# Splitting the q and k weight columns by the halves of the heads' dims, and storing the gate sums from ScalarE's queue, in a hybrid attention block

## The chip, the cores and the metric

The kernel runs on one core of a Trainium2 chip. The metric is the device time of one launch in microseconds; lower is better. Five engines work side by side, each with its own queue of instructions in order: TensorE (PE, matrix products; its weight loads are listed as PEld), VectorE (DVE), ScalarE (ACT), GpSimd (POOL) and SyncE (SP, which here only issues transfers). A transfer is issued by an instruction in an engine's queue (SPq, ACTq) and carried out by 16 DMA engines.

## The reference, cut to what matters

One encoder layer on x of 1024 rows by 1024 columns, all in 32-bit floats. What the change touches is the first product and the rope:

```python
h_in = rms_norm(x, norm_mix_g[l], NORM_EPS)
proj = h_in @ w_in[l]
qa, ka, va, qb, kb, vb, ga, gb = jnp.split(proj, split_idx, axis=-1)
qa = apply_rope(qa.reshape(b, s, A_HEADS, HEAD_DIM), cos, sin)   # the same for ka, qb, kb
...
def apply_rope(t, cos, sin):                                     # heads of 64 dims
    rot = jnp.concatenate([-t4[..., HALF_DIM:], t4[..., :HALF_DIM]], axis=-1)
    out = t4 * cos[None, :, None, :] + rot * sin[None, :, None, :]
```

qa, ka, qb and kb are 512 columns each, the gates ga and gb 1024 each. After that come dilated and differential attention, the gates, an output product, an MLP of 4096 and a last norm; the change leaves these alone but for the addresses from which attention reads q and k.

## The kernel before

Every large product is a Strassen product: a 256-column block of weights is cut into a11, a12, a21, a22 (upper or lower 512 rows of either 128-column half), and seven smaller products of 512 rows replace eight. Each product is twelve matmuls on TensorE (`product`, L245), since every operand is split into a high part (`_h`, made by ScalarE in `halves`, L253) and a low remainder (`_l`, L254, made by GpSimd, or by VectorE for `wd_`), and three of the four cross products are taken. The result is transposed: 128 output columns on the partitions, 1024 rows along the free side.

The change is in stage 1, which makes q, k, v and the gates, and above all in its loop over sixteen items: eight pairs of q or k tiles (`qk_pair`; pairs 8, 12, 10, 14, 0, 4, 2, 6) and eight gates (`gate_rest`; 4, 5, 6, 7, 0, 1, 2, 3), by turns, except that the last four are q2, q6, g2, g3. An item takes five products in `rest_products`. Two go into a double PSUM bank `y` (operands s2 and s4, names `yq` or `yg`), two into a double bank `z` (s1 and s3; `zq`, `zg`), one into a bank of its own (a4; `4q`, `4g`). The pairs 0, 4, 2 and 6 take their two first products (`f0q`, `f1q`) there too, from an operand `wa_q`; those of 8, 12, 10 and 14 (`qk_early`) and of the gates are made elsewhere. The y and the z bank are each there twice, so a bank is taken again two items later, once VectorE has evicted it (L297 for y, L303 for z, L306 for the last).

The operands of one item stand in three buffers per part that go round: `ws_` (s2, s4), `wd_` (s1) and `wt_` (s3, a4). The sums behind them (L273 to L276) are VectorE's, and read the raw columns that SP has loaded two items ahead (L259).

A finished pair goes through `rope` behind the item that follows it in the program. For each of its two tiles, four transfers between blocks of 32 partitions (L501) make the copy `rot` with the halves of every head changed over; then VectorE multiplies rot by the signed sine (L502), GpSimd the tile by the cosine (L503), VectorE adds (L504), ScalarE takes the high part (L512) and VectorE the low (L513), and ScalarE's queue stores both (L514, L515). A finished gate leaves three tiles of sums, `gc`, which SP's queue stores to `gp` (L547), each behind the eviction that completes it. Differential attention begins behind the loop, with SP's loads `kb` and `qb` (L670, L676) and the scores `sb` (L697).

The program order on each engine is not that of the text: a planner of the tile framework puts the instructions of each engine in a row.

Of the kernel before, what the change touches and what calls it, by code (L numbers as in the profile page):

```python
# [37 lines left out]
def shape_tables():  # L38
# [8 lines left out]
    sin_t = np.concatenate([-sin, sin, -sin, sin], 0)  # L47
# [36 lines left out]
def tile_hybrid_block(ctx: ExitStack, tc: tile.TileContext, t: dict, out: bass.AP):  # L84
# [100 lines left out]
    qk_d = [dram(f"qk{j}", [2, P, S]) for j in range(16)]  # L185
# [84 lines left out]
    def rest_operands(name, ra, rb, s1):  # L270

        a11, a12, a21, a22 = ra[:, :DK, :], ra[:, DK:, :], rb[:, :DK, :], rb[:, DK:, :]
# [3 lines left out]
        nc.vector.tensor_tensor(a12, a12, a11, op=ALU.subtract)  # L276
        s2, s4 = halves(ra, f"ws_{name}")
# [218 lines left out]
    def rope(j, raw):  # L496
        scale = -0.125 if j % 8 < 4 else 1.0
        rot = big("xn", f"rot{j}", 2)
        for b in range(4):
            o = b ^ 1  # L500
            nc.sync.dma_start(rot[32 * b:32 * b + 32, :], raw[32 * o:32 * o + 32, :])  # L501
        nc.vector.scalar_tensor_tensor(rot, rot, scale, sin_t, op0=ALU.mult, op1=ALU.mult)  # L502
        nc.gpsimd.tensor_tensor(raw, raw, cos_t, op=ALU.mult)  # L503
        nc.vector.scalar_tensor_tensor(raw, raw, scale, rot, op0=ALU.mult, op1=ALU.add)  # L504
        hi, lo = [big("rh", f"r{z}_{j}", 2, F32R) for z in range(2)]
        if j < 4:

# [18 lines left out]
    def qk_pair(j, raws):  # L526
        xa, xb = [big("x", f"raw{j + a}", 4) for a in range(2)]
        p, u = [p1.tile([P, 512], F32, tag="p1", name=f"{nm}{j}", bufs=4) for nm in ("qp", "qu")]
        if j in EARLY:
            for z, x in enumerate((p, xa[:, 0:512])):  # L530
                nc.sync.dma_start(x, early_d[EARLY.index(j)][z])
        else:
            a11, a12 = halves(raws[0], f"wa_q{j}")
            first_products(f"q{j}", a11, a12, p, xa[:, 0:512])
        operands = rest_operands(f"q{j}", *raws, s1_tile(f"q{j}"))
        rest_products(f"q{j}", operands, p, u, (xa[:, 512:], xb[:, :512], xb[:, 512:]), lambda *_: None)
        return lambda: (rope(j, xa), rope(j + 1, xb))
# [4 lines left out]
    def gate_rest(n, raws):  # L542
        u = p1.tile([P, 512], F32, tag="p1", name=f"gu{n}", bufs=4)
        dst = [p1.tile([P, 512], F32, tag="x", name=f"gc{n}{k}", bufs=4) for k in range(3)]

        def done(a, b, c):
            nc.sync.dma_start(part_d[n][2 * a + b - 1], c)  # L547

        rest_products(f"g{n}", rest_operands(f"g{n}", *raws, s1_tile(f"g{n}")), None, u, dst, done)

    GATES = (4, 5, 6, 7, 0, 1, 2, 3)
    todo = []
    for j, n in zip(EARLY + (0, 4, 2, 6), GATES):
# [46 lines left out]
    def load_qk(jq, jk, half, name):  # L600

        r = slice(64 * half, 64 * half + 64)
        q_src = qk_d[jq][:, r, :].rearrange("z d s -> d z s")
        k_src = [bass.AP(tensor=a.tensor, offset=a.offset, ap=[[S, 64], [0, 2], [1, S]])
                 for a in (qk_d[jk][0, r, :], qk_d[jk][1, r, :])]
# [57 lines left out]
    def b_open(h):  # L663
# [4 lines left out]
        for m in range(2):  # L668
            k = p2q.tile([P, S], F32R, tag="qk", name=f"kb{h}_{m}", bufs=NQK)
            nc.sync.dma_start(f(k), qk_d[12 + h][:, 64 * m:64 * m + 64, :].rearrange("z d s -> d z s"))  # L670
            o.k.append(k)
        for half in range(2):
            for m in range(2):
                q = p2q.tile([P, 2, 512], F32R, tag="qk", name=f"qb{h}_{m}_{half}", bufs=NQK)
                for z in range(2):
                    nc.sync.dma_start(  # L676
                        f(q)[:, z, :], dup(qk_d[8 + h][z, 64 * m:64 * m + 64, 512 * half:512 * half + 512]))
# [789 lines left out]
```

## Time and profile before

| | |
|---|---|
| three runs | 1678.48, 1679.65, 1672.11 us; median 1678.48 |
| the profiled execution, its own time | 1671.93 us, with a span of 1670.1 us |
| granted TensorE clock, mean | 0.974 of full speed |
| TensorE busy in the span | 1560.1 us, 93% |
| VectorE, ScalarE, GpSimd busy | 71%, 42%, 35% |
| stage 1 before the loop; the loop; up to the scores at work | 0 to 139.2; 139.2 to 422.7; 422.7 to 440 us |

How to read it: the table of the loop is the place to look, since nothing else is rewritten. Inside it, the end of each pair's fifth product (the last `4q` matmul) is a mark: the distance from one mark to the next is the time of one pair and one gate. A timeline row gives the start, the duration, the engine, the line, and in brackets the idle time ahead of it and what ended that.

### The profile page before, as it was taken

How to read it: one execution, taken by the hardware profiler on the slowest of the kernel's cores; microseconds unless marked ns; L12 is line 12 of the kernel's file. 1: busy time of each engine (PE TensorE's matmuls, PEld its weight loads, DVE VectorE, ACT ScalarE, POOL GpSimd, SP SyncE). 2: the span in 40 equal slices, each digit the busy share in tenths (PEclk: the TensorE clock that was granted, in tenths of full speed). 3: DMA queues.
4: the chain of work that ended last, by engine and by line, in shares of the span. 5: the costliest groups of instructions: out<-in, count | busy, mean ns of one | idle time of the engine just before them, and what ended most of it. 6: DMA issues, size and time to landing. Idle time of an engine off the chain costs nothing. (4 is left out here: it accounts for less than half of the span.)

```text
span 1670.1 us, 21713 instructions
## 1 busy us (share of the span) xinstructions
PE 1560.1 (93%) x8216; PEld 1319.2 (79%) x8216; DVE 1187.1 (71%) x1383; ACT 698.7 (42%) x1064; POOL 577.1 (35%) x289
## 2 busy tenths in 40 slices
PE   8899889998789997989999999899999998999998
PEld 7798767766677886988878998688888777888876
DVE  5977888699688996655537447644444599899984
ACT  4432222222566873544432326444444552333332
POOL 2644444555232331021220004433333234354551
PEclk9999999999999998999999999999999999999999
DMA  6366576555866657656557332444333561413112
GB/s 230 113 222 199 175 231 201 171 187 158 276 195 212 224 195 269 198 169 216 166 164 277 117 112 88 127 129 130 101 101 114 191 243 46 167 68 124 51 38 101
DMA packets 218488, 271.28 MB, mean 162 GB/s; under 512 B 12784, under 2 KB 145040, under 8 KB 218384
## 3 DMA queue, kind: packets, MB, share of 16 engines
q1 hardware_dynamic: 204560, 236.33, 44.1%
q10 hardware_dynamic: 13824, 33.56, 5.3%
q8 instruction: 65, 1.06, 0.3%
q14 instruction: 39, 0.32, 0.1%
HBM read 183.81 MB, written 80.27 MB: 158 GB/s over the span
## 5 line engine op out<-in xcount | busy, mean ns | idle before, releaser
L1356 PE MATMUL p<-b,a 128*128 128x512 f32 x392 | 155.8, 398 | 5.3 <-DVE b L1272 5.3
L1355 PE MATMUL p<-b,a 128*128 128x512 f32 x392 | 155.3, 396 | 4.4 <-ACT a L1271 4.4
L1357 PE MATMUL p<-b,a 128*128 128x512 f32 x392 | 155.3, 397 | 0.9 <-DVE a L1272 0.9
L1272 POOL TENSOR_TENSOR b<-ws,b 128x1024 fp32r<-128x1024 f32 x27 | 79.1, 2943 | 128.3 <-ACT b L1271 118.3
L1356 PEld LDWEIGHTS p<-b,a 128*128 128x128 f32 x392 | 74.7, 191 | 23.1 <-DVE b L1272 5.7
L1355 PEld LDWEIGHTS p<-b,a 128*128 128x128 f32 x392 | 74.6, 190 | 21.5 <-ACT a L1271 4.9
L1357 PEld LDWEIGHTS p<-b,a 128*128 128x128 f32 x392 | 74.7, 191 | 18.1 <-DVE a L1272 1.5
L697 PE MATMUL sb<-kb,qb 128*128 128x512 f32 x256 | 75.0, 417 | 13.7 <-ACT p L702 8.1
L702 ACT ACTIVATE p<-sb,mn 128x1024 f32<-128x1024 f32 x64 | 71.2, 1115 | 37.4 <-DVE mn L700 23.5
L700 DVE TENSOR_REDUCE mn<-sb 128x1 f32<-128x1024 f32 x64 | 76.8, 1218 | 9.0 <-PE sb L697 8.7
L273 DVE TENSOR_TENSOR s<-w 128x512 f32<-128x512 f32 x15 | 16.9, 1125 | 85.6 <-DMA w<-in_w_ff 85.6
L164 POOL TENSOR_SCALAR n_y<-n_ss 128x1 f32<-128x1 f32 x23 | 6.3, 274 | 188.6 <-ACT n_xn L171 187.1
L811 PE MATMUL sa<-kh_a,zq 128*128 128x256 f32 x256 | 69.1, 301 | 0.9 <-DVE mna L820 0.8
L836 DVE TENSOR_TENSOR pta<-ta,pta 128x512 fp32r<-128x512 f32 x64 | 43.8, 688 | 33.9 <-ACT pta L835 33.8
L1271 ACT ACTIVATE a<-fs 128x1024 fp32r<-128x1024 f32 x28 | 29.4, 1054 | 91.0 <-PE p L1356 64.8
L697 PEld LDWEIGHTS sb<-kb,qb 128*128 128x128 f32 x256 | 46.2, 194 | 26.4 <-ACT p L702 12.4
L811 PE MATMUL sa<-kl_a,zq 128*128 128x256 f32 x256 | 65.9, 288 | 0.0
L254 POOL TENSOR_TENSOR wt_f_l<-w,wt_f_h 128x1024 fp32r<-128x1024 f32 x15 | 36.1, 2405 | 83.7 <-ACT wt_f_h L253 83.7
L1143 ACT ACTIVATE c<-c 128x512 f32<-128x512 f32 x64 | 40.0, 624 | 47.7 <-DVE c L300 35.6
L824 ACT ACTIVATE sm<-sm,mna 128x512 f32<-128x512 f32 x64 | 46.1, 720 | 32.5 <-DVE mna L820 32.0
L835 ACT ACTIVATE pta<-ta 128x512 fp32r<-128x512 f32 x64 | 37.6, 591 | 52.1 <-PE ta L831 44.4
L641 POOL TENSOR_TENSOR gq<-gq,gp 128x512 f32<-128x512 f32 x24 | 36.1, 1533 | 59.4 <-ACT gp L636 59.4
(497 smaller groups left out, 5117.2 us busy)
## 6 DMA issues: line engine op xcount, KB each, us to landing
w<-in_w_in SPq DMA_DIRECT2D x32, 512.0 KB, 4.3
qk<-r ACTq DMA_DIRECT2D x32, 512.0 KB, 5.3
f<-c ACTq DMA_DIRECT2D x64, 256.0 KB, 2.0
rb<-in_w_ff SPq DMA_DIRECT2D x32, 512.0 KB, 5.5
ra<-f SPq DMA_DIRECT2D x64, 256.0 KB, 4.9
w<-in_w_ff SPq DMA_DIRECT2D x30, 512.0 KB, 4.4
vb<-vb SPq DMA_DIRECT2D x16, 512.0 KB, 6.6
rot<-raw SPq DMA_DIRECT2D x64, 128.0 KB, 4.4
```

What stands on the lines that cost most here:

```text
L697: nc.tensor.matmul(sps[:, 512 * n:512 * n + 512], q[:, z, (qb % 4) * P:(qb % 4 + 1) * P], o.k[m][:, 512 * n:512 * n + 512], start=z == 0, ...
L700: nc.vector.tensor_reduce(mn, sps, axis=AX.X, op=ALU.min)
L702: nc.scalar.activation(p, sps, AF.Exp, scale=-1.0, bias=mn, accum_out=o.zz[qb][:, m:m + 1])
L811: nc.tensor.matmul(ps[:, 0:CM], zq[:, n % 4, c, :], kk[:, c * CM:(c + 1) * CM], start=c == 0 and kk is o.kh, stop=c == NCLS - 1 and kk is ...
L824: nc.scalar.activation(sm, sm, AF.Exp, scale=-1.0, bias=mn, accum_out=stat[h % 2][:, n:n + 1])
L835: nc.scalar.activation(view[0], tv, AF.Copy)
L836: nc.vector.tensor_tensor(view[1], tv, f(view[0]), op=ALU.subtract)
L1143: nc.scalar.activation(c, c, AF.Relu)
L1272: eng.tensor_tensor(lo, x, f(hi), op=ALU.subtract)
L1355: nc.tensor.matmul(acc, ah[:, i % 2, c], bh[:, i % 2, :], start=i == 0 and not more, stop=False, skip_group_check=bool(more))
L1356: nc.tensor.matmul(acc, ah[:, i % 2, c], bl[:, i % 2, :], start=False, stop=False, skip_group_check=bool(more))
L1357: nc.tensor.matmul(acc, al[:, i % 2, c], bh[:, i % 2, :], start=False, stop=last, skip_group_check=bool(more))
```

## The change

The raw columns of a pair of q or k tiles were loaded as two blocks of 1024 rows and 128 columns, one for each tile (two heads). They are now loaded as two blocks of 512 rows and 256 columns (four heads), and a tile's operand is picked from them as every other group of 32 columns: `xa` gets the first halves of four heads, `xb` the second halves. The rope then needs no copy between partitions: both tiles are multiplied by sine and cosine, GpSimd making the two products of `xb`, and combined crosswise. The 64 `rot` transfers of 128 KB are gone; the number of arithmetic instructions of a pair's rope stays (VectorE six, GpSimd two, ScalarE two), as does the number of stores. The `rot` tiles are used again for the low parts. In DRAM, q and k rows keep their order head by head, which the stores see to.

With the cut by rows, ws_ now holds s2 and s3, and wt_ holds s4 and a4. The early pairs load 2 blocks of 512 KB instead of one each, 2 MB more in all.

The 24 gate stores are issued by `nc.scalar` instead of `nc.sync`.

```diff
-    sin_t = np.concatenate([-sin, sin, -sin, sin], 0)
+    sin_t = np.concatenate([sin] * 4, 0)
...
-    qk_d = [dram(f"qk{j}", [2, P, S]) for j in range(16)]
+    qk_d = [dram(f"qk{j}", [2, 2 * P, S]) for j in range(8)]
...
+    def qk_raw(j, name, slot):
+        return [v_raw_at(512 * k, qk_col(j), f"{name}{k}", *slot) for k in range(2)]
...
+    def qk_blocks(r):
+        x = r.rearrange("p k (h s i) -> p (k h) s i", s=2, i=32)
+        return [x[:, :, z, :] for z in range(2)]
+    def qk_first(raws, name, eng):
+        hi = wp.tile([P, DC, P], F32R, tag="wh", name=name + "_h", bufs=3)
+        lo = wp.tile([P, DC, P], F32R, tag="wl", name=name + "_l", bufs=3)
+        for k, r in enumerate(raws):
+            x = qk_blocks(r)[0]
+            to_hi, to_lo = [z[:, DK * k:DK * k + DK, :].rearrange("p k (h i) -> p (k h) i", i=32) for z in (hi, lo)]
+            nc.scalar.activation(to_hi, x, AF.Copy)
+            eng.tensor_tensor(to_lo, x, f(to_hi), op=ALU.subtract)
...
+    def qk_halves(r, name):
...
+        x = r.rearrange("p k (h s i) -> p (k h) s i", s=2, i=32)
+        to_hi, to_lo = [z.rearrange("p (s k) (h i) -> p (k h) s i", s=2, i=32) for z in (hi, lo)]
+        nc.scalar.activation(to_hi, x, AF.Copy)
+        nc.gpsimd.tensor_tensor(to_lo, x, f(to_hi), op=ALU.subtract)
...
-    def rope(j, raw):
+    def rope(j, xa, xb):
         scale = -0.125 if j % 8 < 4 else 1.0
-        rot = big("xn", f"rot{j}", 2)
-        for b in range(4):
-            o = b ^ 1
-            nc.sync.dma_start(rot[32 * b:32 * b + 32, :], raw[32 * o:32 * o + 32, :])
-        nc.vector.scalar_tensor_tensor(rot, rot, scale, sin_t, op0=ALU.mult, op1=ALU.mult)
-        nc.gpsimd.tensor_tensor(raw, raw, cos_t, op=ALU.mult)
-        nc.vector.scalar_tensor_tensor(raw, raw, scale, rot, op0=ALU.mult, op1=ALU.add)
...
+        ta, tb = [big("xn", f"rot{j + z}", 2) for z in range(2)]
+        nc.gpsimd.tensor_tensor(tb, xb, sin_t, op=ALU.mult)
+        nc.vector.scalar_tensor_tensor(ta, xa, scale, sin_t, op0=ALU.mult, op1=ALU.mult)
+        nc.gpsimd.tensor_tensor(xb, xb, cos_t, op=ALU.mult)
+        nc.vector.scalar_tensor_tensor(xa, xa, scale, cos_t, op0=ALU.mult, op1=ALU.mult)
+        nc.vector.scalar_tensor_tensor(xa, tb, -scale, xa, op0=ALU.mult, op1=ALU.add)
+        nc.vector.scalar_tensor_tensor(xb, xb, scale, ta, op0=ALU.mult, op1=ALU.add)
+        for y, (raw, rot) in enumerate(((xa, tb), (xb, ta))):
+            hi, lo = big("rh", f"r{y}_{j}", 2, F32R), rot.bitcast(F32R)
...
+            for z, x in enumerate((hi, lo)):
+                nc.scalar.dma_start(qk_d[j // 2][z].rearrange("(h s i) t -> s h i t", s=2, i=32)[y], f(x))
...
-        operands = rest_operands(f"q{j}", *raws, s1_tile(f"q{j}"))
...
+        s2, s3 = qk_halves(raws[0], f"ws_q{j}")
+        (s1,) = halves(s1, f"wd_q{j}", nc.vector)
+        s4, a4 = qk_halves(raws[1], f"wt_q{j}")
...
         def done(a, b, c):
-            nc.sync.dma_start(part_d[n][2 * a + b - 1], c)
+            nc.scalar.dma_start(part_d[n][2 * a + b - 1], c)
```

The planner orders the engines anew. Three places bear on what follows. Numbers in the names are those of pair or gate, then of the buffer; `gu4` is a copy of gate 4's first product, `r0_`, `r1_` are parts of a roped pair.

ScalarE, from gate 4 to pair 12, before:

```order
L253 ACTIVATE ws_q12_h_1729<-w1_20_1589 128x1024
L294 ACTIVATE gu4_1593<-yg4_1614 128x512
L253 ACTIVATE wd_q12_h_1733<-s1_q12_1724 128x512
L253 ACTIVATE wt_q12_h_1737<-w1_21_1591 128x1024
L512 ACTIVATE r0_8_1698<-raw8_1497 128x1024
L514 DMA qk8_80<-r0_8_1698 128x1024
L515 DMA qk8_80<-r1_8_1699 128x1024
L253 ACTIVATE ws_g5_h_1823<-w1_30_1686 128x1024
```

and with the change:

```order
L478 ACTIVATE ws_q12_h_1727<-w1_20_1597 128x16x2x32
L302 ACTIVATE gu4_1601<-yg4_1622 128x512
L557 ACTIVATE r0_8_1706<-raw8_1505 128x1024
L557 ACTIVATE r1_8_1711<-raw9_1506 128x1024
...
L597 DMA gp4_1493<-gc40_1602 128x512
L560 DMA qk4_76<-r1_8_1711 4x32x1024
L597 DMA gp4_1493<-gc42_1604 128x512
L597 DMA gp4_1493<-gc41_1603 128x512
L560 DMA qk4_76<-rot8_1698 4x32x1024
L259 ACTIVATE wd_q12_h_1731<-s1_q12_1722 128x512
L478 ACTIVATE wt_q12_h_1735<-w1_21_1599 128x16x2x32
```

`wd_q12_h` and `wt_q12_h`, which stood ahead of the rope's parts, now stand behind them and behind the three stores of gate 4; the third of these carries `gc41`, which the last eviction of gate 4 completes. It is the same at gates 5 and 6.

ScalarE, from gate 7 to pair 0, before:

```order
L294 ACTIVATE gu7_2256<-yg7_2277 128x512
L253 ACTIVATE ws_q0_h_2422<-w1_80_2252 128x1024
L253 ACTIVATE wd_q0_h_2426<-s1_q0_2417 128x512
L512 ACTIVATE r0_14_2361<-raw14_2160 128x1024
L514 DMA qk14_86<-r0_14_2361 128x1024
L515 DMA qk14_86<-r1_14_2362 128x1024
L266 ACTIVATE qp0_2383<-f0q0_2389 128x512
L253 ACTIVATE wt_q0_h_2430<-w1_81_2254 128x1024
```

and with the change:

```order
L468 ACTIVATE wa_q0_h_2353<-w1_80_2230 128x512
L302 ACTIVATE gu7_2234<-yg7_2255 128x512
...
L560 DMA qk7_79<-r1_14_2344 4x32x1024
L597 DMA gp7_1496<-gc70_2235 128x512
L560 DMA qk7_79<-rot14_2331 4x32x1024
L597 DMA gp7_1496<-gc72_2237 128x512
L597 DMA gp7_1496<-gc71_2236 128x512
L272 ACTIVATE qp0_2351<-f0q0_2359 128x512
L478 ACTIVATE ws_q0_h_2392<-w1_80_2230 128x16x2x32
L259 ACTIVATE wd_q0_h_2396<-s1_q0_2387 128x512
L478 ACTIVATE wt_q0_h_2400<-w1_81_2232 128x16x2x32
```

All three operands of the pair's last five products, which stood partly ahead of the rope's stores, stand behind the third gate store (`gc71`). It is the same at gates 0 and 1 with pairs 4 and 2.

VectorE, from gate 4's first eviction to its last, before (`zg4`, `4g4` are the banks that are evicted):

```order
L297 TENSOR_TENSOR gc40_1594<-yg4_1614,gu4_1593 128x512
L275 TENSOR_TENSOR w1_30_1686<-s1_g5_1818,w1_30_1686 128x512
L276 TENSOR_TENSOR w1_30_1686<-w1_30_1686 128x512
L254 TENSOR_TENSOR wd_q12_l_1734<-s1_q12_1724,wd_q12_h_1733 128x512
L502 SCALAR_TENSOR_TENSOR rot8_1690<-rot8_1690,sin_t_1478 128x1024
L300 TENSOR_TENSOR gc40_1594<-zg4_1615,gc40_1594 128x512
L302 TENSOR_TENSOR gc41_1595<-zg4_1615,gu4_1593 128x512
L504 SCALAR_TENSOR_TENSOR raw8_1497<-raw8_1497,rot8_1690 128x1024
L513 TENSOR_TENSOR r1_8_1699<-raw8_1497,r0_8_1698 128x1024
L303 TENSOR_TENSOR gc42_1596<-zg4_1615,gc41_1595 128x512
L306 TENSOR_TENSOR gc41_1595<-4g4_1616,gc41_1595 128x512
L502 SCALAR_TENSOR_TENSOR rot9_1704<-rot9_1704,sin_t_1478 128x1024
```

and with the change (`L548`, `L547`, `L558` are the combinations and the low parts of the rope of pair 8):

```order
L546 SCALAR_TENSOR_TENSOR raw8_1505<-raw8_1505,cos_t_1485 128x1024
L548 SCALAR_TENSOR_TENSOR raw9_1506<-raw9_1506,rot8_1698 128x1024
L547 SCALAR_TENSOR_TENSOR raw8_1505<-rot9_1699,raw8_1505 128x1024
L305 TENSOR_TENSOR gc40_1602<-yg4_1622,gu4_1601 128x512
...
L558 TENSOR_TENSOR rot9_1699<-raw8_1505,r0_8_1706 128x1024
L558 TENSOR_TENSOR rot8_1698<-raw9_1506,r1_8_1711 128x1024
...
L308 TENSOR_TENSOR gc40_1602<-zg4_1623,gc40_1602 128x512
L310 TENSOR_TENSOR gc41_1603<-zg4_1623,gu4_1601 128x512
...
L314 TENSOR_TENSOR gc41_1603<-4g4_1624,gc41_1603 128x512
L281 TENSOR_TENSOR w1_30_1694<-w1_30_1694 128x512
L260 TENSOR_TENSOR wd_q12_l_1732<-s1_q12_1722,wd_q12_h_1731 128x512
```

Before, one tile of pair 8 was roped ahead of gate 4's last eviction (`4g4`) and one behind it; now both tiles are roped ahead of it, and so ahead of `zg4` too. `wd_q12_l`, which stood ahead of the rope, now follows the last eviction.

## Rows read from the trace of the kernel before

**Rows 1.** Windows: length, busy us by engine, PEclk, DMA share, GB/s.

```profile
0.00:139.20 139.20, 123.67 (x852) 113.46 (x853) 105.94 (x107) 59.70 (x88) 59.06 (x43) 0.98 0.56 183
139.20:422.70 283.50, 259.73 (x1057) 203.39 (x1058) 234.35 (x214) 71.05 (x81) 139.08 (x52) 0.96 0.62 194
154.98:252.45 97.47, 87.75 (x361) 68.35 (x359) 82.70 (x75) 23.25 (x26) 46.67 (x18) 0.96 0.64 197
252.45:361.10 108.65, 103.35 (x434) 82.11 (x434) 88.07 (x83) 27.37 (x32) 53.37 (x21) 0.98 0.59 184
361.10:386.40 25.30, 21.86 (x85) 16.36 (x83) 20.27 (x19) 6.19 (x7) 16.72 (x7) 0.93 0.48 150
386.40:422.70 36.30, 30.99 (x121) 23.93 (x122) 34.50 (x29) 9.44 (x11) 16.29 (x7) 0.91 0.58 196
```

**Rows 2.** Timeline, TensorE: pair 8's fifth product begins; gate 4's first follows it.

```profile
152.03 0.63 PE L245 MATMUL 4q<-hT,wt_q_h 128*128 128x512 f32 x2
...
154.83 0.63 PE L245 MATMUL yg<-hT,ws_g_h 128*128 128x512 f32 x2
```

**Rows 3.** Timeline, TensorE: gate 4's last matmul, and the stall in pair 12.

```profile
168.59 0.40 PE L245 MATMUL 4g<-hT,wt_g_l 128*128 128x512 f32 x1
...
179.02 1.19 PE L245 MATMUL zq<-hT,wd_q_h 128*128 128x512 f32 x2 [4.43 <-DVE gc L303]
```

**Rows 4.** Timeline, VectorE: the last eviction of gate 4, behind a tile's rope.

```profile
178.98 0.69 DVE L306 TENSOR_TENSOR gc<-4g,gc 128x512 f32<-128x512 f32 x1
```

**Rows 5.** Timeline: gate 0's last matmul and its last eviction, no rope ahead.

```profile
306.36 0.39 PE L245 MATMUL 4g<-hT,wt_g_l 128*128 128x512 f32 x1
...
308.61 0.69 DVE L306 TENSOR_TENSOR gc<-4g,gc 128x512 f32<-128x512 f32 x1
```

**Rows 6.** Timeline, ScalarE: splits of operands, and a wait at a store.

```profile
168.84 1.07 ACT L253 ACTIVATE wt_q_h<-w 128x1024 fp32r<-128x1024 f32 x1 [4.96 <-PE 4g L245]
...
178.31 0.33 ACTq L515 DMA_DIRECT2D qk<-r  x1
178.76 1.06 ACT L253 ACTIVATE ws_g_h<-w 128x1024 fp32r<-128x1024 f32 x1 [3.11 <-DMA qk<-r]
...
196.22 0.58 ACT L294 ACTIVATE gu<-yg 128x512 f32<-128x512 f32 x1
198.06 0.63 ACT L253 ACTIVATE wd_q_h<-s_q 128x512 fp32r<-128x512 f32 x1 [1.26 <-PE zg L245]
```

**Rows 7.** Timeline: VectorE instructions alone, and one beside a GpSimd instruction.

```profile
168.79 0.69 DVE L276 TENSOR_TENSOR w<-w 128x512 f32<-128x512 f32 x1
...
190.79 2.41 POOL L254 TENSOR_TENSOR wt_g_l<-w,wt_g_h 128x1024 fp32r<-128x1024 f32 x1 [7.76 <-ACT wt_g_h L253]
191.19 2.57 DVE L276 TENSOR_TENSOR w<-w 128x512 f32<-128x512 f32 x1
...
238.59 1.21 DVE L504 SCALAR_TENSOR_TENSOR raw<-raw,rot 128x1024 f32<-128x1024 f32 x1
```

**Rows 8.** Groups of the loop: busy us, mean ns, idle ahead of them, releasers.

```profile
L503 POOL TENSOR_TENSOR raw<-raw,cos_t 128x1024 f32<-128x1024 f32 x16 | 43.9, 2749 | 15.9 <-DMA rot<-raw 13.9 <-DVE raw L504 1.2 <-DVE s_g L273 0.7
```

**Rows 9.** Page, transfers: count, KB each, median us from issue to landing.

```profile
rot<-raw SPq DMA_DIRECT2D x64, 128.0 KB, 4.4
```

**Rows 10.** The tile gp: issue of one store in ns, min, median, max.

```profile
L547 SPq DMA_DIRECT2D gp<-gc x24: 319/339/592, 171.8 to 426.4; - x24
```

**Rows 11.** Timeline: TensorE's stalls in the last two gates and at the scores.

```profile
396.47 1.19 PE L245 MATMUL zg<-hT,wd_g_h 128*128 128x512 f32 x2 [4.12 <-DVE raw L303]
...
424.54 0.54 SPq L547 DMA_DIRECT2D gp<-gc  x1
...
429.68 1.19 PE L697 MATMUL sb<-kb,qb 128*128 128x512 f32 x2 [5.66 <-DMA qb<-qk]
```

**Rows 12.** Timeline ahead of the loop: an early pair's low part, and a product waiting.

```profile
66.59 2.41 POOL L254 TENSOR_TENSOR wa_e_l<-wqe,wa_e_h 128x1024 fp32r<-128x1024 f32 x1
...
75.91 0.72 PE L245 MATMUL f1e<-hB,wa_e_h 128*128 128x512 f32 x2 [3.10 <-DVE s_ec L268]
```

More of the change, by code (lines that the diff above doesn't have):

```diff
@@ L183, in dram, with qk_rows @@
         return dr.tile(shape, dt, tag=name, name=name)
-    qk_d = [dram(f"qk{j}", [2, P, S]) for j in range(16)]
+    qk_d = [dram(f"qk{j}", [2, 2 * P, S]) for j in range(8)]
+    def qk_rows(j, half, z=slice(0, 2)):
+        r = 128 * (j % 2) + 64 * half
+        return qk_d[j // 2][z, r:r + 64, :]
     va_d = [dram(f"va{g}", [S, 4, P]) for g in range(2)]
@@ L532, in qk_pair @@
         else:
-            a11, a12 = halves(raws[0], f"wa_q{j}")
+            a11, a12 = qk_first(raws, f"wa_q{j}", nc.gpsimd)
             first_products(f"q{j}", a11, a12, p, xa[:, 0:512])
-        operands = rest_operands(f"q{j}", *raws, s1_tile(f"q{j}"))
-        rest_products(f"q{j}", operands, p, u, (xa[:, 512:], xb[:, :512], xb[:, 512:]), lambda *_: None)
-        return lambda: (rope(j, xa), rope(j + 1, xb))
+        (a11, a21), (a12, a22) = [qk_blocks(r) for r in raws]
+        s1 = s1_tile(f"q{j}")
+        rest_sums(a11, a12, a21, a22, s1.rearrange("p k (h i) -> p (k h) i", i=32))
+        s2, s3 = qk_halves(raws[0], f"ws_q{j}")
+        (s1,) = halves(s1, f"wd_q{j}", nc.vector)
+        s4, a4 = qk_halves(raws[1], f"wt_q{j}")
+        rest_products(f"q{j}", (s1, s2, s3, s4, a4), p, u, (xa[:, 512:], xb[:, :512], xb[:, 512:]), lambda *_: None)
+        return partial(rope, j, xa, xb)
     part_d = [dram(f"gp{n}", [3, P, 512]) for n in range(8)]
@@ L546, in done, with gate_raw @@
         def done(a, b, c):
-            nc.sync.dma_start(part_d[n][2 * a + b - 1], c)
+            nc.scalar.dma_start(part_d[n][2 * a + b - 1], c)
         rest_products(f"g{n}", rest_operands(f"g{n}", *raws, s1_tile(f"g{n}")), None, u, dst, done)
+    def gate_raw(n, name, slot):
+        return [col_raw(w_in, 3072 + 256 * n + P * a, f"{name}{a}", *slot) for a in range(2)]
     GATES = (4, 5, 6, 7, 0, 1, 2, 3)
@@ L553, in tile_hybrid_block, with load_raws @@
     for j, n in zip(EARLY + (0, 4, 2, 6), GATES):
-        todo += [(partial(qk_pair, j), qk_col(j)), (partial(gate_rest, n), 3072 + 256 * n)]
+        todo += [(partial(qk_pair, j), partial(qk_raw, j)), (partial(gate_rest, n), partial(gate_raw, n))]
     todo = todo[:13] + todo[14:15] + todo[13:14] + todo[15:]
-    raws = [raw_pair(w_in, todo[n][1], f"w1_{n}", SLOTS) for n in range(2)]
+    def load_raws(n):
+        turn1[0] ^= 1
+        return todo[n][1](f"w1_{n}", SLOTS[turn1[0]])
+    raws = [load_raws(n) for n in range(2)]
     ropes = []
@@ L600, in load_qk @@
     def load_qk(jq, jk, half, name):
-        r = slice(64 * half, 64 * half + 64)
-        q_src = qk_d[jq][:, r, :].rearrange("z d s -> d z s")
+        q_src = qk_rows(jq, half).rearrange("z d s -> d z s")
         k_src = [bass.AP(tensor=a.tensor, offset=a.offset, ap=[[S, 64], [0, 2], [1, S]])
-                 for a in (qk_d[jk][0, r, :], qk_d[jk][1, r, :])]
+                 for a in (qk_rows(jk, half, 0), qk_rows(jk, half, 1))]
         tiles = []
@@ L676, in b_open @@
                     nc.sync.dma_start(
-                        f(q)[:, z, :], dup(qk_d[8 + h][z, 64 * m:64 * m + 64, 512 * half:512 * half + 512]))
+                        f(q)[:, z, :], dup(qk_rows(8 + h, m, z)[:, 512 * half:512 * half + 512]))
                 o.q[m, half] = q
```

36 lines of the change are left out of this document (21 added, 15 removed).

## The prediction

> **What bounds the kernel now.** I read the windows first. The loop takes 283.5 us; TensorE is busy for 259.7 of them at a clock of 0.96, and VectorE for 234.4 [rows 1]. A fifth product runs from 152.03 to 154.83, 2.80 us or 0.233 us for each of twelve matmuls [rows 2], so the loop's 88 products (16 items by five, and two more for four pairs) need 246.4 us; 37 us of the loop are stalls and slower matmuls. One pair and one gate need 28.0 us in the first half, 33.6 us in the second. The three rounds from 154.98 to 252.45 take 97.5, 32.5 each; the next three, to 361.10, take 108.7, 36.2 each [rows 1]. So rounds have 4.5 and 2.6 us of loss, and a change can give back no more than that in one, but can add without limit.
>
> The timeline names the loss. Gate 4's products end at 168.59 + 0.40 = 168.99, and pair 12 stalls at 179.02 for 4.43 us until VectorE has evicted the z bank at L303 [rows 3]. The last eviction of that gate starts at 178.98 [rows 4], 10.0 us after its product was done, with half a rope and more ahead of it on VectorE. At gate 0, with no rope ahead, it is 308.61 − 306.75 = 1.9 us [rows 5]. So **VectorE's place in line** sets the stalls. It is late because it shares time with GpSimd: the same VectorE instruction with two operands in SBUF takes 0.69 us by itself and 2.57 us when it starts 0.40 us after a GpSimd instruction of 2.41 us [rows 7]. It ends 0.56 us behind the GpSimd one, which is about its own duration. I count such instructions of the two engines one behind the other; evictions from PSUM, 0.6 us apart in a row, stay short.
>
> **The 64 transfers that go.** GpSimd waits 13.9 us of the loop on them [rows 8], each lands 4.4 us after issue [rows 9]. None of this is a stall of TensorE as such; it delays the rope, which delays VectorE's evictions. Arithmetic counts per pair are equal, so VectorE and GpSimd save no work. What the removal is worth is then seen only in the order, next.
>
> **The order, rounds of pairs 12, 10 and 14.** With the change both tiles of a rope stand ahead of the gate's last eviction on VectorE, and the third gate store waits for that eviction in ScalarE's queue, ahead of wd_q and wt_q. That a store in ScalarE's queue holds what follows it is in the trace: the store at 178.31 waits for its low part, and the split behind it starts at 178.76 after 3.11 us of idling [rows 6]. wd_q and wt_q feed 48 of the pair's 60 matmuls. From the end T of the pair before, up to the last eviction, VectorE has four multiply-adds of the rope and two low parts at 1.14 us (start to start; the row has 1.21 [rows 7]), four weight sums at 0.6, six evictions at 0.6: 6.8 + 2.4 + 3.6 = 12.8 us. GpSimd has two rope products and two low parts at 2.4: 9.6. One behind the other that is T + 22.4. Before, the same eviction came at 178.98 − 154.98 = T + 24.0, so the sum is of the right size, and the eviction is no earlier than it was; what is new is that ScalarE waits for it. Then the eviction 0.7, the store's issue 0.34 [rows 10], wd_q 0.6, wt_q 1.07 [rows 6], its low part on GpSimd 2.4: T + 27.5. Eight matmuls can run before that low part arrives; 40 by 0.233 follow, 9.3, and 0.6 for slower matmuls after the stall: before, the first after such a pause took 1.19 us for a pair, where 0.63 is usual [rows 2, 3]. That is 37.4 us a round, 112.2 for three; the first has three more weight sums ahead of it, 1.8. Against 97.5: **+16.5**.
>
> **The order, rounds of pairs 0, 4 and 2.** Here ws_q, wd_q and wt_q all stand behind the third store; TensorE has only the gate's five products and the two first ones, 19.6 us, to go on with. The eviction at T + 23.6 (two weight sums more), itself 0.7, issue 0.34, a copy of the first product 0.58, ws_q 1.07 and its low part 2.4: T + 28.7. Then 58 matmuls, 13.5, and 1.4 for slower ones after a wait of 9 us: 43.6 us a round, 130.8 against 108.7: **+22.1**.
>
> **The end of the loop.** From 361.10 to 386.40 only seven products run, with 25.3 us for 19.6, and no gate; I take 1.5 back (0 to 3). In the last two gates no pair follows the stores. They lose 4.12 us at 396.47 to a late eviction [rows 11] and 8.3 in all (36.3 against 28.0 [rows 1]); with the rope done earlier I take 4 back (0 to 5). Then the first scores wait 5.66 us on qb, whose issues on SP alternate with gate stores that wait for their sums [rows 11]. Those leave SP's queue, and with no rot issues either SP can load kb and qb up to that pair early: the wait goes, **−6** (−2 to −6). Together −11.5.
>
> **Ahead of the loop.** 2 MB more are loaded and the splits of early pairs read 32-column groups. Where a wa_e low part takes 2.41 us and products wait up to 3.10 us on other work [rows 12], I take +2, between 0 and +8 (four pairs by 2 us). That GpSimd is as fast on groups of 32 elements isn't shown by the trace; two such instructions in each of eight pairs and a half-size pair at four. I take nothing, as VectorE's and ScalarE's shuffled writes in the last pairs' ropes are no slower; the other end, 2.41 to 3.5 us at twelve places on the path, is +13. Reading 1 KB runs in place of 512 B when loading could make loads quicker; they wait in no term above, so nothing.
>
> **Sum.** 16.5 + 22.1 − 11.5 + 2 = +29.1 on the profiled execution's 1671.9: 1701. The profile is the lowest of the runs but for 0.2 us, and their median is 6.6 above it; a median of the new kernel should lie a few us above what I summed, so 1704.
>
> **The stores by a rule.** The rows say that ScalarE idled 3.11 us behind a store which waited for its data [rows 6]. The Trainium skill, "DMA: Bandwidth & Descriptors", section "Issuing engines are not separate DMA queues", states that starting transfers on several engines only saves the sequencer's time to initiate them, usually small. By it the move would be worth 24 × 0.34 = 8 us of issuing, off TensorE's path, and no wait; the row agrees that the issue is small, and speaks against counting only that.
>
> **Rivals.**
> *The stores cost ScalarE only their issue.* If the last evictions come before ScalarE gets to the stores (VectorE then runs the rope beside the GpSimd work rather than behind it, some 6 us sooner in each round), wd_q and wt_q are ready by T + 20 and the second kind's ws_q likewise. A first-kind round takes 33.5 (+1.0), a second-kind one 35.0 (−1.2); with −11.5 and +2 that is about −10: 1662 by the profile, 1665 as a median. Against it: the order itself, and an eviction late by 10.0 us [rows 3, 4]. Chance 0.12.
> *VectorE on time, faster by more.* Without waits on rot transfers the rope fits into the time the gate's products take, and every gate is evicted as gate 0's was, 1.9 us late [rows 5]. Rounds lose 2.2 and 1.6 us less than now, −11.4, with −9.5: 1651, or 1654. For it: 13.9 us of waits that go [rows 8]. Against it: 22.4 us of work in a line where the gate's products take 14. Chance 0.08.
> *It comes to nothing.* VectorE's line is shorter by 4 to 5 us than I sum, as the evictions need no port and can run beside GpSimd (six by 0.6), and the rounds then lose 2 to 3 us each, which the end of the loop gives back: 1672 to 1685, 1678 in the middle. Chance 0.14.
> *Worse: the early pairs and GpSimd's groups at their upper ends.* +6 and +13 on the sum: 1723. Chance 0.10.
>
> **How the numbers follow.** The forecast, 1704 with its own range of 1690 to 1715, has 0.56. What a measurement of this kernel can tell from no change is about 0.5%, 8 us. Slower by more: 0.56 + 0.10 = 0.66. Within: 0.14. Faster: 0.12 + 0.08 = 0.20. The range leaves out the second rival, the lower end of the first and a little beyond the last: 1660 to 1722, which is wide since the faster case hangs on one wait that the trace of before can't show: ScalarE's at the gate stores.
>
> **What would show it.** Right: in the loop, ScalarE's wd_q and wt_q behind gates 4 to 6, and ws_q behind 7, 0 and 1, idle until a gp store, which starts with VectorE's last gate eviction some 22 to 25 us into the round; TensorE stalls in every pair for 5 to 9 us on ws_q, wd_q or their low parts; rounds of 37 and 43 us; no wait of the first scores on qb. Wrong: rounds at or under 32.5 and 36.2 us; an eviction within 5 us of its product; a stall that names a transfer; ScalarE idle before the splits ended by something other than a store. A loss ahead of the loop of over 8 us, or GpSimd instructions of over 3 us without VectorE beside them, would mean that the change of layout costs what I have put at nothing.

## The result, and the profile after

| | before | after |
|---|---|---|
| median of the runs measured side by side | 1675.3 us | 1783.9 us (1783.3 to 1788.6) |
| ratio, 95% interval | | 1.0666 (1.0635 to 1.0696) |
| profiled execution: own time, span | 1671.93, 1670.1 | 1783.39, 1781.6 |
| granted TensorE clock, mean | 0.974 | 0.947 |
| TensorE busy in the span | 1560.1 us, 93% | 1590.9 us, 89% |

Slower, as forecast, but by 108.6 us where the sum said 29, and outside the range. The windows between the same marks as in [rows 1] say where (start:end, length, then busy us with instruction counts of PE, PEld, DVE, ACT and POOL, granted clock, DMA share, GB/s):

```profile
0.00:161.04 161.04, 143.47 (x912) 128.94 (x913) 113.85 (x118) 65.00 (x97) 64.14 (x47) 0.94 0.62 197
161.04:308.32 147.28, 95.88 (x362) 73.48 (x361) 81.30 (x77) 23.64 (x27) 49.40 (x18) 0.83 0.42 137
308.32:452.79 144.47, 115.51 (x434) 88.24 (x432) 91.56 (x86) 27.66 (x36) 61.55 (x25) 0.87 0.33 104
452.79:480.60 27.81, 22.50 (x85) 17.81 (x84) 25.15 (x24) 6.83 (x8) 13.28 (x5) 0.88 0.22 62
480.60:527.70 47.10, 33.18 (x121) 24.32 (x119) 15.58 (x18) 7.72 (x9) 15.09 (x7) 0.86 0.29 101
...
187.00:189.00 2.00, 0.00 (x0) 0.00 (x0) 0.00 (x0) 0.00 (x0) 0.00 (x0) 0.50 0.25 93
```

The rounds of pairs 12, 10, 14 took 147.28 us for 97.47, those of 0, 4, 2 took 144.47 for 108.65, and the last two gates 47.10 for 36.30. In the first three rounds VectorE, GpSimd and ScalarE did about the work of [rows 1] (81.30, 49.40, 23.64 us). So most of it is waiting. A smaller part is slower matmuls: TensorE is busy 95.88 us for 87.75 in these rounds, with 362 matmuls for 361, at a granted clock of 0.83 for 0.96. The clock falls where TensorE stands idle, to 0.50 (its lower level, 1.2 GHz) in the last row. Over the whole span TensorE is busy 30.8 us longer with the same 8216 matmuls. The last row shows what stands there: two microseconds in which no engine computes, while the DMA engines are busy for a quarter and move 93 GB/s.

The timeline of the same round, with ScalarE's queue, VectorE's last eviction of gate 4 (L314) and TensorE's next product (start, duration, engine; in brackets the idle time ahead and what ended it; issues, ACTq, count as idle):

```profile
178.35 1.09 ACTq L560 DMA_DIRECT2D qk<-r  x1
...
179.61 0.52 ACTq L560 DMA_DIRECT2D qk<-rot  x1
...
181.95 1.16 ACTq L597 DMA_DIRECT2D gp<-gc  x1
...
183.20 1.65 ACTq L560 DMA_DIRECT2D qk<-r  x1
...
184.23 0.68 DVE L314 TENSOR_TENSOR gc<-4g,gc 128x512 f32<-128x512 f32 x1
184.95 5.27 ACTq L597 DMA_DIRECT2D gp<-gc  x2
...
196.35 0.53 ACTq L560 DMA_DIRECT2D qk<-rot  x1
196.93 0.63 ACT L259 ACTIVATE wd_q_h<-s_q 128x512 fp32r<-128x512 f32 x1 [17.65 <-DMA gp<-gc]
...
197.61 0.79 PE L251 MATMUL zq<-hT,wd_q_h 128*128 128x512 f32 x1 [16.66 <-ACT wd_q_h L259]
```

The last eviction starts 184.23 − 161.04 = 23.2 us into the round; the forecast had T + 22.4, and 24.2 with the first round's 1.8. Then the gate's third store could go and `wd_q_h` follow 0.34 us later. It began 12.0 us after the eviction was done (196.93 − 184.91). The issues themselves, 0.34 us in [rows 10], take 0.5 to 3.9 (the row of 5.27 us is two issues, of 3.91 and 1.26); behind the last pair of them ScalarE stands for another 6 us ahead of the fourth q/k store. TensorE waits 16.66 us. The waiting is not on the *data* of a store any more but on the stores.

### The profile page after: what moved, and what is told of

It is laid out like the page before. It is cut to its first block, busy times and chain, and to the rows that moved or that the text cites. A ratio compares the mean times of both kernels' runs of the same rounds, so it can differ in the third digit from the quotient of the medians.

```text
span 1781.6 us, 21588 instructions
## 1 busy us (share of the span) xinstructions
PE 1590.9 (89%) x8216; PEld 1337.1 (75%) x8216; DVE 1178.8 (66%) x1385; ACT 699.5 (39%) x1072; POOL 574.4 (32%) x295
## 5 line engine op out<-in xcount | busy, mean ns | idle before, releaser
L1413 PEld LDWEIGHTS p<-b,a 128*128 128x128 f32 x392 | 74.7, 191 | 22.9 <-DVE b L1329 5.7
L757 DVE TENSOR_REDUCE mn<-sb 128x1 f32<-128x1024 f32 x64 | 76.7, 1216 | 11.3 <-PE sb L754 10.7
L759 ACT ACTIVATE p<-sb,mn 128x1024 f32<-128x1024 f32 x64 | 71.3, 1116 | 21.9 <-DVE mn L757 21.7
L893 DVE TENSOR_TENSOR pta<-ta,pta 128x512 fp32r<-128x512 f32 x64 | 43.7, 688 | 32.0 <-ACT pta L892 31.8
L251 PE MATMUL yq<-hT,ws_q_h 128*128 128x512 f32 x64 | 30.4, 570 | 32.4 <-ACT ws_q_h L478 18.4
L251 PE MATMUL zq<-hT,wd_q_h 128*128 128x512 f32 x64 | 24.2, 455 | 36.8 <-ACT wd_q_h L259 36.8
```

The source lines that it names most:

```text
L251: nc.tensor.matmul(acc, w[wz][:, k, :], hb[nm][hz][:, k, :], start=k == 0 and wz + hz == 0, stop=k == DK - 1 and wz == 1)
L757: nc.vector.tensor_reduce(mn, sps, axis=AX.X, op=ALU.min)
L759: nc.scalar.activation(p, sps, AF.Exp, scale=-1.0, bias=mn, accum_out=o.zz[qb][:, m:m + 1])
L893: nc.vector.tensor_tensor(view[1], tv, f(view[0]), op=ALU.subtract)
L1413: nc.tensor.matmul(acc, ah[:, i % 2, c], bl[:, i % 2, :], start=False, stop=False, skip_group_check=bool(more))
```

## The experiments

Besides the cause, two things were open: which half of the change does it (the layout, or the queue of the gate stores), and, when both were mended, what remained. "Rounds" below are the two sums of three rounds, 97.47 and 108.65 us before and 147.28 and 144.47 after.

### The form of the q and k stores

One line of the changed kernel is edited; every engine keeps its order:

```diff
-                nc.scalar.dma_start(qk_d[j // 2][z].rearrange("(h s i) t -> s h i t", s=2, i=32)[y], f(x))
+                nc.scalar.dma_start(qk_d[j // 2][z][P * y:P * y + P, :], f(x))
```

> The changed kernel, but each q or k store writes its 128 rows to 128 rows that follow one another, instead of to four groups of 32 rows; this leaves out the order of the heads' rows, so the scores are of permuted dims. The instructions and their order on every engine are those of the changed kernel. Theory S (the grouped stores land in 13 to 25 us where straight ones landed in 3 to 4, they fill ScalarE's DMA queue, and the gate stores and operand splits behind them wait): rounds of 37 and 43 us as forecast, wd_q of pair 12 within 2 us of the last eviction of gate 4, total 1690 to 1715. Theory O (the order alone: the wait for VectorE's last eviction in ScalarE's queue costs all of it): no change, 1775 to 1790.

Measured: 1706.5 us, 1.0235 of before (1.0192 to 1.0279); its profiled execution 1707.81. All three marks of theory S are met: rounds of 38.7 and 43.1 us, 1.8 us to `wd_q_h`, and the total. Of the 111 us between the profiled executions of the change and of the kernel before, 75.6 go with this line. Windows:

```profile
158.63:274.85 116.22, 92.67 (x361) 71.94 (x360) 84.10 (x83) 23.66 (x27) 50.35 (x18) 0.90 0.50 172
274.85:404.12 129.27, 109.44 (x433) 84.86 (x432) 87.50 (x84) 28.74 (x37) 61.89 (x26) 0.92 0.33 115
404.12:428.13 24.01, 21.31 (x86) 16.87 (x85) 23.28 (x19) 6.00 (x7) 13.90 (x5) 0.93 0.37 132
428.13:461.47 33.34, 30.07 (x122) 23.54 (x120) 21.98 (x20) 7.73 (x9) 17.17 (x6) 0.95 0.52 189
...
182.00:187.00 5.00, 2.39 (x6) 1.86 (x7) 1.46 (x3) 1.58 (x2) 1.42 (x1) 0.50 1.04 404
```

and the same places in its timeline:

```profile
175.60 0.34 ACTq L560 DMA_DIRECT2D qk<-r  x1
...
181.00 1.53 ACTq L597 DMA_DIRECT2D gp<-gc  x2
...
181.49 0.68 DVE L314 TENSOR_TENSOR gc<-4g,gc 128x512 f32<-128x512 f32 x1
...
183.56 0.33 ACTq L560 DMA_DIRECT2D qk<-rot  x1
183.93 0.63 ACT L259 ACTIVATE wd_q_h<-s_q 128x512 fp32r<-128x512 f32 x1 [7.40 <-DMA gp<-gc]
...
184.61 0.79 PE L251 MATMUL zq<-hT,wd_q_h 128*128 128x512 f32 x1 [6.39 <-ACT wd_q_h L259]
```

From the end of the eviction to `wd_q_h` it is now 1.8 us in place of 12.0, an issue takes 0.33 to 0.43 again, and while stores and loads move all 16 DMA engines are busy (share 1.04, 404 GB/s). The kernel has the same number of stores with the same bytes; only the DRAM side's shape differs, [128 rows] against [4 groups][32 rows].

Is it the number of groups, or that the rows are not in one block? Two more kernels change only the number of groups, i=8 (16 groups of 8 rows; the dims are permuted alike in q and k, so the scores keep their sums) and i=64 (2 groups of 64 rows):

```diff
-                ...rearrange("(h s i) t -> s h i t", s=2, i=32)[y], f(x))
+                ...rearrange("(h s i) t -> s h i t", s=2, i=8)[y], f(x))     # the other kernel: i=64
```

> The changed kernel with its q and k stores in 16 groups of 8 rows with gaps between, instead of 4 groups of 32 (this permutes the dims of the scores, since the rows go to other places). Order and sizes are those of the changed kernel, gate stores on ScalarE's queue. Theory C (the number of groups in the outermost dimension decides over how many of the 16 DMA engines a store is spread; four groups use few): 16 groups land like straight rows, in 3 to 8 us, and the total is 1700 to 1715 as with straight rows. Theory G (gaps between groups make a store slow in themselves): no better than the changed kernel, 1770 or more.

Measured: 1713.9 us, 1.0270 (1.0235 to 1.0305), as theory C had it.

> The same with 2 groups of 64 rows (the rows' order is left out here too). Theory C: half as many DMA engines as with four groups, so a store lands in about twice the time, 25 to 50 us, and the total is 1840 to 2000. Theory G: fewer gaps, 1710 to 1785.

Measured: 1903.8 us, 1.1417 (1.1384 to 1.1449). A window of that kernel in which no engine computes:

```profile
184.00:187.00 3.00, 0.00 (x0) 0.00 (x0) 0.00 (x0) 0.00 (x0) 0.00 (x0) 0.50 0.13 53
```

The count of groups it is: straight 1706, 16 groups 1714, 4 groups 1784, 2 groups 1904. A share of 0.13 is 2 engines of 16, and 0.25 in the changed kernel is 4. A store in 4 groups is carried by four DMA engines, one in 2 groups by two, at 23 to 27 GB/s each (93/4, 53/2). A pair stores four times 512 KB; at 93 GB/s that is 22.5 us of a round of 32 to 36.

The trace's semaphore counts agree. A semaphore is a counter that a transfer steps when it lands, and the trace records every step. A straight store makes 16 steps when it lands, and so does one in 16 groups. One in 4 groups makes one step 0.4 us after its issue and four when it lands; one in 2 groups one and two. By the last step, the 32 q/k stores of before are complete 2.6 to 8.0 us after the start of their issue (median 3.8), those of the changed kernel after 10.1 to 21.7 us (14.7; the "13 to 25" of theory S was read wrongly), those of 16 groups after 3.7 to 8.3 (4.4), those of 2 groups after 12.8 to 33.2 (24.7).

The gate stores behind them, of ordinary shape, are complete after 5.8 to 18.9 us (median 15.2), before after 2.0 to 7.5 (2.9). Their steps show why: of the 16 of the gate store issued at 184.95 us, twelve come after 5.9 to 6.9 us and four after 16.5 to 18.5. A sixteenth of it is queued on each of the four busy engines.

This is the rule that I should have weighed. The Trainium skill, "DMA: Bandwidth & Descriptors", section "Why a DMA increments its semaphore by 16 and not by 1", says that a transfer is spread over the largest number of engines, at most 16, that divides the slowest dimension of size over 1 of both its sides. By it 4 groups give 4 engines, 2 give 2, and 16 groups or 128 straight rows give all 16; the trace's shares agree with each (0.25, 0.13, and 1.04 for both of the last), and so do the four, two and 16 steps at landing.

### The queue of the gate stores

The changed kernel with the gate sums back on SP's queue, the stores still in groups:

```diff
-            nc.scalar.dma_start(part_d[n][2 * a + b - 1], c)
+            nc.sync.dma_start(part_d[n][2 * a + b - 1], c)
```

> The changed kernel with the gate stores issued by SP again; q and k stores stay grouped. Theory S: the four grouped stores of a pair still stand ahead of wd_q and wt_q in ScalarE's queue and the fourth still waits for a place, so rounds stay above 36 us and the total is 1700 to 1750. Theory O: ScalarE waits for no gate eviction any more, and the total is 1655 to 1675, as before or under it.

Measured: 1773.9 us, 1.0627 (1.0589 to 1.0666). That is at most 10 us better than the change, whose interval it touches (1.0635 to 1.0696), and against both expectations: the grouped stores need no gate store beside them to do harm. Timeline of that kernel, and below it one line of the list of waits (engine, tile, line, what it waited for: us in all, times, longest):

```profile
182.12 5.46 ACTq L560 DMA_DIRECT2D qk<-rot  x1
187.63 0.63 ACT L259 ACTIVATE wd_q_h<-s_q 128x512 fp32r<-128x512 f32 x1 [9.48 <-issue]
188.32 1.22 PE L251 MATMUL zq<-hT,wd_q_h 128*128 128x512 f32 x2 [8.49 <-ACT wd_q_h L259]
```

```profile
DVE s_q L278 <- DMA w<-in_w_in: 75.8, 6, 18.0
```

They act in three ways. ScalarE is held in the issue of its own fourth q/k store, 5.46 us. SP's loads of weights, which spread over all engines, land late since four of these are busy: of the 16 steps of the load issued at 334.75 us twelve come within 4.6 us, four after 13.0 to 16.3. And SP's queue stands itself until grouped stores of ScalarE's queue are complete. SP's own list of waits, from 139 to 460 us, has 62 us on them, among them these two rows (L597 is a gate store, L265 a load of weights); in the next kernel it has none.

```profile
SPq L597 <- DMA qk<-r: 15.8, 3, 7.9
SPq L265 <- DMA qk<-rot: 13.3, 3, 5.9
```

VectorE's sums waited 75.8 us for loads of weights; in the next kernel, with straight stores, 12.9. How much of that each of the last two ways makes, no run separates.

Both edits, straight stores and gate sums on SP:

> Straight q and k stores (the order of the heads' rows is left out) and the gate stores on SP. Both theories: neither the grouped stores nor the gate evictions hold ScalarE, 1650 to 1672. If it stays over 1690, a third cause is in the new layout of the weights or in the rope's new place on VectorE.

Measured: 1688.1 us, 1.0109 (1.0073 to 1.0145), between the two marks of the expectation and 1% over before, so a third cause was left. Against straight stores with gate sums on ScalarE, 1706.5, the queue is worth 18 us. Its windows and three rows of its TensorE timeline in pair 12:

```profile
157.90:271.68 113.78, 94.00 (x362) 72.31 (x361) 89.89 (x83) 23.67 (x27) 50.67 (x18) 0.91 0.52 177
271.68:389.66 117.98, 107.53 (x434) 83.88 (x432) 84.31 (x84) 28.75 (x37) 62.22 (x26) 0.96 0.36 126
```

```profile
174.61 0.73 PE L251 MATMUL yq<-hT,ws_q_h 128*128 128x512 f32 x2 [2.55 <-DVE gc L305]
...
180.59 1.19 PE L251 MATMUL zq<-hT,wd_q_h 128*128 128x512 f32 x2 [2.90 <-DVE gc L311]
...
184.46 0.80 PE L251 MATMUL zq<-hT,wd_q_l 128*128 128x512 f32 x1 [2.68 <-DVE wd_q_l L260]
```

Rounds 12, 10, 14 hardly gain (116.22 to 113.78); 0, 4, 2 gain 11.3. What is left in the first three is VectorE: TensorE waits for its evictions (L305, L311) and for its low part, all behind the rope.

The queue alone, in the kernel before (the opposite edit of the same line):

> The kernel before, with only the gate stores moved to ScalarE's queue. Theory S: straight stores, so ScalarE waits a few us at the second and third gate store of each round at most, and what stands behind these (the next gate's ws) has slack: 1670 to 1690. Theory O: the move of the stores alone costs most of the loss, over 1710.

Measured: 1669.4 us, 0.9985 (0.9962 to 1.0007): theory S, at the lower edge of its range. ScalarE does wait for gate stores there too (8.0, 7.0 and 2.2 us in the list of its waits), and the rounds shift: 93.9 us for 97.47 in the first three, 116.4 for 108.65 in the next, 19.5 for 25.3 in that of pair 6. But the last gate ends at 423 us as before, so in total the queue costs nothing there. And gate sums on SP with 16 groups:

> The changed kernel with two lines edited: stores of q and k in 16 groups of 8 rows, gate stores issued by SP again. By theory C the stores land like straight ones, so this is the run with both edits over again without its rows left out of order: 1682 to 1700, some 17 us over before, all of it in rounds of about 38 and 39 us. If it comes out at or under the kernel before, the rest of the loss in the run with both edits came from something else than the order on VectorE.

Measured: 1688.7 us, 1.0093 (1.0075 to 1.0111), the same as straight stores. All in one table (us, ratio to before):

| stores of q and k | gate sums on SP | gate sums on ScalarE |
|---|---|---|
| kernel before, straight | 1 | 1669 (0.9985) |
| changed, straight | 1688 (1.0109) | 1706 (1.0235) |
| changed, 16 groups | 1689 (1.0093) | 1714 (1.0270) |
| changed, 4 groups | 1774 (1.0627) | **1784 (1.0666)** |
| changed, 2 groups | not run | 1904 (1.1417) |

### The order of VectorE's work

Another way to straight stores: q and k lie in DRAM by halves of dims, and the loads of attention pick a head's two halves with two transfers each (64 more); gate sums on SP.

> The changed kernel with q and k kept in DRAM by halves, so that every store is straight, and loads of a head's two halves split in two (64 loads more in the attention stages); gate stores on SP. The same order in the loop as the run with both edits: 1680 to 1695, with at most 5 us for the extra loads. If loads in two halves of 64 partitions are slow in the way of the grouped stores, attention loses over 10 us.

Measured: 1700.1 us, 1.0196 (1.0160 to 1.0232), some 12 us over straight stores without the extra loads: these cost more than I expected. The profile puts it in differential attention, where the scores `sb` take 211 us from first to last for 198; what in it waits for the loads I didn't follow. On this kernel the rope's second half was put behind the next gate: the crosswise additions and the low parts may only be placed behind that gate's last eviction, and the gate sums get buffers of their own.

```diff
+        return partial(rope_end, j, xa, xb, ta, tb)
+    def rope_end(j, xa, xb, ta, tb):          # the crosswise additions, splits and stores
...
+        with tc.issue_after(getattr(ins, "ins", ins)):     # ins: L314 of the gate
+            fn()
```

> As the last, and the crosswise additions and low parts of a rope are queued on VectorE behind the gate's last eviction; the gate sums take 512-column buffers of their own instead of those of the raw pairs, since the third had to wait for a roped tile. If the rope's place ahead of the evictions is what is left of the loss (rounds of 38.0 and 39.3 us with both edits), rounds fall to 29 to 32 and 34 to 36, and the total to 1645 to 1662. If VectorE and GpSimd have no room for the layout as such, it stays over 1675.

Measured: 1697.5 us, 1.0170 (1.0134 to 1.0206), far over what was expected. The first three rounds took 95.7 us, less than before, and as expected; the next three 46.2, 41.5 and 39.7. Waits of TensorE from 160 to 400 us:

```profile
PE yq L251 <- ACT wt_q_h L479: 7.7, 3, 3.0
PE yq L251 <- POOL wt_q_l L480: 7.2, 6, 4.6
```

ScalarE now had the rope's splits ahead of `wt_q`. So the next kernel (16 groups, gate sums on SP) puts the rope's end behind the pair's `wt_q` split as well:

```diff
+        with tc.issue_after(getattr(ins, "ins", ins)), tc.issue_after(getattr(split[0], "ins", split[0])):
```

> The last, with the crosswise additions and the low parts of the rope queued on VectorE behind the gate's last eviction and the rope's splits queued on ScalarE behind the pair's wt split; gate sums have 512-column buffers of their own. If the rope's place on VectorE and ScalarE is all that is left of the loss: rounds of 30 to 33 and 34 to 37 us, no wait of the first scores over 2 us, 1648 to 1668, as before or a little under it. If the layout as such costs (early loads, GpSimd on 32-element groups), it stays over 1675.

Measured: 1676.5 us, 1.0028 (1.0012 to 1.0045). The rounds came near what was expected (30 to 34 and 34 to 37 us), the total did not. Its loop is over at 417.33 us (before, 422.70), but the first scores then wait for the last pairs' ropes, now late, and their stores and loads:

```profile
444.47 3.75 PE L773 MATMUL sb<-kb,qb 128*128 128x512 f32 x8 [17.71 <-DMA qb<-qk]
```

With the last two pairs roped in place (`if n < 13: ends.append(fn)`, `else: fn()`):

> The last version of the changed kernel, but the ropes of the last two pairs (2 and 6) run in place, with no queueing behind a gate, so that q and k are stored and their buffers are free before the last gate ends. In the run before, the loop ended 5 us earlier than in the kernel before, and then the first scores waited 17.7 us on qb. If that wait was owed to the late ropes alone: the wait falls under 3 us, the scores begin at 418 to 426 us of the span instead of 444, and the total is 1650 to 1664, under both kernels. If the loads of q and k wait for something else, it stays over 1670.

Measured: 1666.2 us against 1668.4 of before beside it, 0.9987 (0.9968 to 1.0007); no difference that can be told. The wait and the start of the scores came as expected, the gain on both kernels did not. Windows, and the first scores, which began at 429.68 before [rows 11]:

```profile
160.56:256.37 95.81, 88.69 (x361) 69.06 (x360) 81.04 (x79) 23.39 (x26) 47.13 (x18) 0.96 0.60 202
256.37:361.99 105.62, 101.83 (x433) 80.72 (x432) 87.24 (x86) 29.16 (x37) 61.02 (x26) 1.00 0.47 149
```

```profile
422.63 1.63 PE L777 MATMUL sb<-kb,qb 128*128 128x512 f32 x6 [2.04 <-DMA qb<-qk]
```

The last experiment asks whether the order would have helped without the new layout, in the kernel before, with its rot transfers. It has the order of the kernel that took 1676.5 us, in which the last two ropes are late too:

> The kernel before, with its rot transfers, its gate stores on SP and its layout, and only the order of the last run: the rope's addition and low part behind the gate's last eviction, gate sums in buffers of their own. If VectorE's place in line was the loss of the kernel before too: rounds of 29 to 31 and 34 to 35.5 us, 1650 to 1666. If the transfers between partitions set the rounds: no gain, 1665 to 1680.

Measured: 1691.6 us, 1.0110 (1.0091 to 1.0129), over both expectations. The first three rounds take 105.95 us for 97.47, and TensorE waits for evictions again:

```profile
187.66 1.19 PE L245 MATMUL yg<-hT,ws_g_h 128*128 128x512 f32 x2 [3.90 <-DVE raw L301]
```

The next three take 108 us, as before, and the loop is over at 427 us (before, 423). Most of the loss is not in the loop but in the late ropes of the last pairs:

```profile
456.83 3.75 PE L722 MATMUL sb<-kb,qb 128*128 128x512 f32 x8 [27.54 <-DMA qb<-qk]
```

The first scores wait 27.54 us on qb, for 5.66 before. So the loop gains nothing by this order with the transfers, while with the layout it is over at 417.33 us in place of 450 (16 groups, gate sums on SP, 1.0093). In totals, both with late last ropes, the order costs 1.1% with the transfers and gives 0.65% with the layout (1.0093 to 1.0028); the last step, to 0.9987, is the last pairs roped in place, which was not run with the transfers. That the order shortens the loop with the split layout, and not with the transfers, is shown; why the first rounds lose by it with the transfers, beyond the wait above, I didn't follow.

## Why the prediction was right in direction and wrong in size

The sum, term by term, beside the kernel with straight stores (e1), which is the change without the one thing the sum lacked, and the changed kernel (us against before, from the windows):

| term | forecast | straight stores | changed kernel |
|---|---|---|---|
| ahead of the loop's first round | +2 | +3.7 | +6.1 |
| rounds of pairs 12, 10, 14 | +16.5 | +18.8 | +49.8 |
| rounds of pairs 0, 4, 2 | +22.1 | +20.6 | +35.8 |
| round of pair 6 | −1.5 | −1.3 | +2.5 |
| last two gates | −4 | −3.0 | +10.8 |
| from the last gate to the first scores | −6 | −7.0 | +1.3 |
| to the first scores | +29.1 | +31.8 | +106.3 |

- **The step that failed** is the cost of the stores. The prediction put "the store's issue 0.34 [rows 10]" behind the last eviction, and the grouped q/k stores, equal to those of before in number and bytes, at nothing. The rows that the order fences of the change print as 4x32x1024 were in view; their first dimension, 4, was what mattered. With that form, 12.0 us lie between the eviction's end and `wd_q_h`, where the sum has 0.34. The largest error, 74.5 us to the first scores, is this one line.
- **Rounds 12, 10, 14**: the size is met when the stores are straight, T + 22.9 for the last eviction (181.49 − 158.63), and a stall of 6.39 us on `wd_q_h`, among the 5 to 9 that were said. But the reason was half wrong. With the gate sums on SP, where ScalarE waits for none of them, 113.78 of the 116.22 us remain: VectorE's own line, its evictions and `wd_q_l` behind the rope, is as late as ScalarE's. I had counted one of two equal limits, so that the term came out is in this part luck.
- **Rounds 0, 4, 2**: here the store in ScalarE's queue was the limit: 129.27 with it, 117.98 without (forecast 130.8).
- **End of the loop and first scores**: −1.5, −4 and −6 were right with straight stores and were all eaten by the grouped ones; in the changed kernel the last gates lose 10.8 and the first scores wait 8.06 us on qb for their 5.66.
- **The rival "the stores cost ScalarE only their issue"** is refuted by 18 us between the kernels with gate sums on either queue, both straight. "VectorE on time" needs the order of the last kernels; as planned it doesn't come. The Trainium skill's sentence in "DMA: Bandwidth & Descriptors", section "Issuing engines are not separate DMA queues", that the choice only saves the usually small time to start a transfer, agrees with the total of the kernel before (0.9985). It says nothing of the 18 us of waiting behind the stores in the change's order.
- **"Worse"** was built on the early pairs and on GpSimd's groups of 32. Ahead of the loop 6.1 us were lost, 3.7 with straight stores. GpSimd's split of `ws_q` with such groups took 2596 ns on average, 2541 before, hardly more; an early pair's split is now two of half the size, 1536 ns each, for one of 2388.
- **The signs.** ScalarE's `wd_q_h` idle until "DMA gp<-gc" is the wait that the prediction had named as a sign for itself, but 17.65 us long, and most of it behind issues and stores already on their way, not behind VectorE. Against it speak rounds of 49 and 48 us for its 37 and 43, and the scores' wait on qb.

The 6 us in which ScalarE stands ahead of its fourth store with no issue running (190.2 to 196.35) end with an earlier store of the pair. The fourth store waits for the semaphore on which the pair's second store, issued at 179.61, counts, and starts 0.02 us after that store's last step. So it does in two more kernels: with straight stores the last step comes at 183.54 us and the fourth store starts at 183.56, after 1.0 us of standing; with 2 groups these are 203.93 and 203.95. What stays open is why a single issue takes up to 3.9 us while four engines are busy.

## What to carry to other kernels

Before a store's access pattern is rearranged, look at its outermost dimension: with 2 and 4 groups there, as many DMA engines carried it here, with 16 all of them. Equal bytes and equal count are not equal cost. And where a transfer between partitions is removed, plan again what waited for it: here the layout with stores over all engines cost 1%, and with the rope put behind the evictions, the last pairs' apart, it gave that back, with no gain over the kernel before.

## What the hardware showed that I had not expected

- An issue on ScalarE's queue is not a constant: 0.33 us at the median with straight stores, up to 4.97 for a gate store behind stores in four groups. With two groups it is up to 9.70 us for a q/k store and 18.17 for a gate store (rows of the issues, ns as min/median/max; the first is of the changed kernel, the others of the one with two groups). An engine with work of its own is held as long.

```profile
L597 ACTq DMA_DIRECT2D gp<-gc x24: 326/1230/4972, 181.9 to 537.9; - x24
```

```profile
L560 ACTq DMA_DIRECT2D qk<-rot x16: 500/502/9701, 178.1 to 625.8; - x16
L597 ACTq DMA_DIRECT2D gp<-gc x24: 326/5684/18166, 180.4 to 659.0; - x24
```

- A store that uses four DMA engines slows transfers of other queues, since each has a share on those four: four of a load's 16 steps came 13.0 to 16.3 us after its issue, the others within 4.6, and VectorE waited 75.8 us for weight loads in place of 12.9.
- The 16-group form, which uses all engines, still takes 0.53 us to issue where straight rows take 0.33; with the gate sums on SP the two kernels take the same (1.0093 and 1.0109), and with them on ScalarE the intervals of 1.0270 and 1.0235 overlap.
